# A kernel's start in finer slices, and five small moves of work behind it

## The chip, the cores and the metric

The kernel runs on one core of a Trainium2 chip. The metric is the device time of one execution in microseconds (us). Five engines are named below: PE (TensorE, the matmuls; PEld is its loading of weights), DVE (VectorE), ACT (ScalarE), POOL (GpSimd) and SP (SyncE, which here issues most of the loads). Each engine runs its own instruction list in order and waits on semaphores for the others.

## The reference, cut to what matters

The program is a two-layer backbone over 256 context tokens and 256 latent tokens of D = 1024 features. Layer 0 mixes tokens with a bidirectional chunkwise mLSTM, layer 1 with multi-head latent attention (MLA); each is followed by a gated convolutional feed-forward block (ConvFFN, 2816 features). Every sub-layer reads a modulated input and ends in a layer norm:

```python
def _modulation(cond, w, b):
    m = jax.nn.silu(cond) @ w + b
    return jnp.split(m[:, None, :], 6, axis=-1)

h = x * (1 + scale) + shift
x = _layer_norm(ALPHA * x + gate * sublayer(h), ln_g, ln_b)
```

The latent tokens are modulated by `c`, the context tokens by `c_ctx`, so there are two condition rows. The first product of all is `h @ m_w_up` (1024 x 2048 features for each of 512 tokens), and it needs `SiLU(c) @ ada_w`, a product with 1024 x 2048 weights (shift and scale), before its first operand exists. All arithmetic is fp32.

## The kernel before, in words

**Products.** A product in fp32 accuracy is three matmuls (`mm3`, lines 391 to 393): each operand is split in `hi`, its value rounded to the matmul type fp32r by a copy on ACT, and `lo = src - hi`, a subtraction on DVE; the sum is hi.hi, hi.lo, lo.hi. Activations are held by features on the 128 partitions with tokens along the row, in eight tiles of 128 features for D (`hT[k]`). Weights come through a ring (class `Stream`): SP loads raw tiles of 512 KB (`raw`), ACT casts them (line 330), DVE subtracts (line 333), and a use of the ring hands over the pair. The plan (`_plan`) fixes the order of the weights.

**What sets the order.** Outside the start the framework's scheduler orders each engine's instructions with the kernel's own generators in the background: `bg` is stepped by `tick` and finished by `drain`, `bg2` is a second list with the modulation of the later sub-layers, and `late` holds generators that `take_late` appends to `bg`. Their place in the text, and where a `yield` lets the product in front go on, is what moves work.

**The start** (`start_up`, within `manual_schedule`). `LOADS` is the order of the loads on SP: `a` is a group of modulation weights, `x` a group of tokens by feature tiles (`tokT`), `r` a whole weight tile of `m_w_up` (one tile of 128 output features, all 1024 input features). `STEPS` is the order of work on PE, DVE and ACT at once, one letter a step:
- `S`: cast and subtract one tile of modulation weights (`ada_split`, lines 396 and 397). `A`: its matmuls, with `SiLU(c)` and `SiLU(c_ctx)` as the four columns of a small operand (`condr`, hi and lo) against 512 columns of weights, line 472, result `adar`, four rows.
- `C`: copy of the rows; `T`: transposes of them to columns, line 484, result `adat`; `O`: bias added, giving shift and scale by partition (`mod0`).
- `E`: modulation of one feature tile of tokens (`mod_tile`); `H`: its split in hi and lo (`hT`).
- `W`: split of half a weight tile of `m_w_up`; `V` k m: the three matmuls of feature tile k into output tile m, 512 tokens wide, lines 391 to 393, result `up`. 8 x 5 of them are in the start (`NUP` = 5 output tiles), 120 matmuls.
- `D` n: n matmuls on zeros into a spare bank (line 664, result `idle`).

`GROUPS` says which feature tiles share one round of `A C T O`; before there are four groups of two. The small constants (`sm`) are loaded ahead of all in one transfer of 227 KB. `w_up` then goes on with the other 11 output tiles.

**The end of layer 0** (`w_fout0`). The second FFN product of layer 0 is built from partial products that are added on DVE (`u2`, `p5`, `p6`, `p7`, in PSUM and SBUF), lines 1436 to 1443 in two stages, while the last six weight tiles are split (line 333) and their operands `fz` are formed (line 1384).

**Layer 1's attention** (`mla`). The layer norm's output `z` is transposed (`ln_T`, line 1196, result `zT`), scaled with shift and scale by partition (line 1203 on ACT for even tiles, line 1205 on DVE for odd ones, result `zm`), and split (1208 and 1209, result `hl`). With `hl` PE makes the key-value rows `dkv` and the query rows `dq`; both get an RMS norm (`rms`, whose last scaling, line 1512, is on DVE). At the same time the norm's gain and bias are multiplied into `z` for the residual (`ln_x`, lines 1224 and 1225, from `late`), and the keys and values of the context, `kn` and `v`, are made and split.

**The second FFN** (`after0`, then `ffn_in`). The norm after the attention goes the same way, `ln_rows` (1168, 1170), `ln_T`, result `h`. `ffn_in` takes the pair of each weight against `h`: the hi weight against hi and lo of `h` side by side in 512 columns (a view `both` with hi and lo in two places of a tile), the lo weight against the 256 hi columns, in turn for each of the eight feature tiles (line 1317).

## Time and profile before

| what | value |
|---|---|
| median of three executions | 1374.81 us (1374.66 to 1375.21) |
| the profiled execution | 1372.7 us, of which 1370.9 us are its span |
| PE busy | 1346.8 us, 98% of the span; 24.1 us not busy |
| DVE, ACT, POOL busy | 1077.0, 720.9, 121.5 us |
| granted TensorE clock, mean | 0.998 of full speed |
| bytes moved | 297.58 MB, mean 217 GB/s |

The span is from the first to the last instruction that the hardware profiler saw in one execution; the profiled execution's own time holds a little more, before and behind. A row of the timeline reads: start and length in us, engine, line, operation, result <- operands, shape, how many in a row, and in brackets the idle time before it with what ended it. A row of the waits reads: who waited, for what, then us in total, times and the longest. Matmuls overlap: a length in a row is the time from a matmul's start to its modelled end, so the pace is the distance of two starts.

### The profile page before, as it was taken

What the parts mean: (1) busy time and instruction counts of PE and PEld (TensorE: products, weight loads), DVE (VectorE), ACT (ScalarE), POOL (GpSimd) and SP (SyncE); (2) the same over time, 40 slices, a digit from 0 to 9 for tenths busy, and PEclk for the clock granted to TensorE, in tenths of its full rate; (3) what the DMA queues carried; (4) which work ended last, traced back from release to release, by engine and by line L of the source; (5) the groups of instructions that cost most, each with busy time, mean ns of one, the idle gap of its engine ahead of it and who ended that gap; (6) DMA issues with size and microseconds to landing.
All of it is one profiled execution on the core that took longest, in us unless ns stands there. A gap on an engine that the chain in (4) does not pass through costs nothing.

```text
span 1370.9 us, 18618 instructions
## 1 busy us (share of the span) xinstructions
PE 1346.8 (98%) x6581; PEld 1121.5 (82%) x6581; DVE 1077.0 (79%) x1748; ACT 720.9 (53%) x1242; POOL 121.5 (9%) x215
## 2 busy tenths in 40 slices
PE   7999999999999999999999999999999999999997
PEld 3788888888788888888898888888878898888886
DVE  7699757677588696897979978767888889788873
ACT  6675444445544455464643343333557667466660
POOL 0122000011011011030001000000001001000100
PEclk9999999999999999999999999999999999999999
DMA  9789848789666363786627877745987436366760
GB/s 337 242 304 331 275 158 247 236 291 297 216 197 210 108 231 123 248 277 242 204 97 240 301 244 224 226 144 202 310 267 238 138 101 216 102 187 189 252 199 31
DMA packets 97900, 297.58 MB, mean 217 GB/s; under 512 B 12136, under 2 KB 24808, under 8 KB 97808
## 3 DMA queue, kind: packets, MB, share of 16 engines
q1 hardware_dynamic: 68672, 218.52, 48.4%
q0 software_dynamic: 17472, 57.57, 13.4%
q10 hardware_dynamic: 11664, 20.32, 4.1%
q8 instruction: 51, 0.84, 0.2%
q14 instruction: 41, 0.34, 0.1%
HBM read 262.90 MB, written 33.46 MB: 216 GB/s over the span
## 4 chain that ended last, share of the span: by engine, by line
PE 92%; DVE 3%; DMA 2%; ACT 1%; issue 1%; ACTq 0%; SPq 0%; DVEq 0%
PE fin L1317 8%; PE fin L392 6%; PE fin L391 6%; PE fin L393 6%; PE tok L391 6%; PE tok L392 6%; PE tok L393 6%; PE y L392 6%; PE y L393 6%; PE y L391 6%; PE qk L391 4%; PE qk L393 4%; PE qk L392 4%; PE up L391 2%; PE up L392 2%; PE up L393 2%
## 5 line engine op out<-in xcount | busy, mean ns | idle before, releaser
L333 DVE TENSOR_TENSOR w<-raw,w 128x1024 fp32r<-128x1024 f32 (+2 forms) x286 | 343.1, 1202 | 146.3 <-ACT w L330 141.5
L330 ACT CAST w<-raw 128x1024 fp32r<-128x1024 f32 (+2 forms) x286 | 296.2, 1037 | 287.9 <-PE tok L393 79.6
L512 DVE SCALAR_TENSOR_TENSOR junk<-ar,bc 128x1024 f32<-128x1024 f32 x128 | 155.7, 1216 | 4.7 <-ACT bc L554 2.4
L392 PE MATMUL fin<-h,w 128*128 128x512 f32 (+1 forms) x376 | 141.2, 376 | 0.0
L393 PE MATMUL fin<-h,w 128*128 128x512 f32 (+1 forms) x376 | 140.9, 375 | 0.0
L391 PE MATMUL fin<-h,w 128*128 128x512 f32 (+1 forms) x376 | 140.8, 376 | 0.1
L1317 PE MATMUL fin<-h,w 128*128 128x256 f32 (+1 forms) x640 | 112.9, 339 | 0.0
L1317 PEld LDWEIGHTS fin<-h,w 128*128 128x128 f32 x640 | 98.1, 189 | 14.6
L391 PE MATMUL qk<-xc,w 128*128 128x512 f32 x256 | 100.7, 393 | 0.0
L393 PE MATMUL qk<-xc,w 128*128 128x512 f32 x256 | 99.9, 390 | 0.0
L392 PE MATMUL qk<-xc,w 128*128 128x512 f32 x256 | 99.8, 390 | 0.0
L392 PEld LDWEIGHTS fin<-h,w 128*128 128x128 f32 x376 | 70.8, 188 | 13.1 <-DVE h L1209 0.2
L391 PEld LDWEIGHTS fin<-h,w 128*128 128x128 f32 x376 | 70.6, 188 | 13.2 <-ACT h L1208 0.3
L393 PEld LDWEIGHTS fin<-h,w 128*128 128x128 f32 x376 | 70.8, 188 | 12.6
L391 PEld LDWEIGHTS qk<-xc,w 128*128 128x128 f32 x256 | 48.1, 188 | 10.0 <-issue 0.4
L393 PEld LDWEIGHTS qk<-xc,w 128*128 128x128 f32 x256 | 48.1, 188 | 9.9
L392 PEld LDWEIGHTS qk<-xc,w 128*128 128x128 f32 x256 | 48.1, 188 | 9.7
L391 PE MATMUL up<-hT,w 128*128 128x512 f32 x128 | 50.3, 393 | 0.1
L392 PE MATMUL up<-hT,w 128*128 128x512 f32 x128 | 50.0, 390 | 0.3 <-DVE hT L397 0.3
L393 PE MATMUL up<-hT,w 128*128 128x512 f32 x128 | 49.9, 390 | 0.0
L391 PE MATMUL tok<-w,hT 128*128 128x512 f32 x128 | 49.8, 389 | 0.0
L392 PE MATMUL tok<-w,hT 128*128 128x512 f32 x128 | 49.8, 389 | 0.0
(456 smaller groups left out, 3160.1 us busy)
## 6 DMA issues: line engine op xcount, KB each, us to landing
raw<-in_ws SPq DMA_DIRECT2D x287, 512.0 KB, 4.6
ar<-in_adaT SPq DMA_DIRECT2D x80, 512.0 KB, 4.7
adaw<-in_ada_w SPq DMA_DIRECT2D x32, 256.0 KB, 6.2
t2d<-raw ACTq DMA_DIRECT2D x13, 512.0 KB, 5.6
raw<-t2d SPq DMA_DIRECT2D x13, 512.0 KB, 5.3
raw<-in_ws POOLq DMA_DIRECT2D x13, 512.0 KB, 7.5
zr<-fd ACTq DMA_DIRECT2D x33, 128.0 KB, 4.2
xmd<-xr POOLq DMA_DIRECT2D x16, 256.0 KB, 4.6
```

The lines of the kernel that those rows point to most:

```text
L330: k.nc.scalar.copy(h[:, :cols], src)
L333: k.nc.vector.tensor_sub(l[:, :cols], src, h[:, :cols])
L391: mm(out, w[0], x[0], start=start, stop=False, skip_group_check=on)
L392: mm(out, w[0], x[1], start=False, stop=False, skip_group_check=on)
L393: mm(out, w[1], x[0], start=False, stop=stop, skip_group_check=on)
L512: nc.vector.scalar_tensor_tensor(o, w, 1.0, self.bc[j], op0=ALU.mult, op1=ALU.mult, accum_out=col[:, k, j:j + 1])
L1317: nc.tensor.matmul(o, a, b, start=k == 0 and i == 0, stop=k == 7 and i == 1)
```

## The change

In the start:
- Modulation weights and the first five output tiles of `m_w_up` are laid out on the host as whole tiles in the order of use: `ada0`, 16 tiles of 128 x 1024 with whole rows, and `up0`, eight tiles, one for each feature tile k, holding its 128 rows times the 640 columns of the five output tiles. Before, the modulation weights were read with rows of 1 KB out of the full matrix, and the five `m_w_up` tiles came one output tile at a time.
- `GROUPS` is (0), (1), (2, 3), (4, 5), (6, 7): the first two feature tiles have rounds of their own, of two tiles (S, A) each, with matmuls of 256 columns instead of 512. `A` is now the hi half of a tile's matmuls and `B` the lo half.
- Only 32 columns of the constants (the conditions and the modulation bias, `sm0`) are loaded ahead; the rest (`s`) comes behind the second weight slice.
- `W` k splits one slice of 640 columns; `V` k m reads its columns. `LOADS` and `STEPS` are written anew, with ten matmuls on zeros ahead of all (`WARM`) in place of the seven in `D4` and `D3`. The ring starts with output tile 5.

Behind it:
- `w_fout0`: the second stage of the sums is a background generator, stepped by the ticks of the last six weight tiles, instead of standing ahead of them.
- layer 1's norm before the attention: all eight scalings of `ln_T` on ACT (`both=False`). `rms`: the last scaling on ACT. `ln_x` is taken up behind the `dkv` product, no longer ahead of `mla`, and the step of the background that stood there is gone.
- layer 1's norm before the second FFN: `ln_T4`. The eight transposes of the first token tile go ahead, then five matmuls on a weight into a spare bank, then the eight transposes of the second; scalings alternate by pairs between ACT and DVE, each followed by its cast and subtraction, and nothing else of it is issued ahead of the first one.
- `ffn_in` of layer 1: seven matmuls with hi weights (512 columns), eight with lo weights (256 columns), and the last hi one, instead of in turn. hi and lo of `h1` lie side by side, so that the 512 columns are one run.

What PE does from the start to the first product of `w_up` (rows with a count are instructions in sequence; `adar` the modulation rows, `adat` their transposes, `idle` the matmuls on zeros, `up` the product, `w` its weights). Before:

```order
L472 MATMUL adar<-adas,condr 4x512 x16
L664 MATMUL idle<-zero 128x512 x4
L484 MATMUL adat<-ident,adarow 128x4 x4
L472 MATMUL adar<-adas,condr 4x512 x16
L664 MATMUL idle<-zero 128x512 x3
L391 MATMUL up<-hT,w 128x512
L392 MATMUL up<-hT,w 128x512
L393 MATMUL up<-hT,w 128x512
```

And now:

```order
L627 MATMUL idle<-zero 128x512 x10
L487 MATMUL adar<-adas,condr 4x256 x16
L500 MATMUL adat<-ident,adarow 128x4 x2
L487 MATMUL adar<-adas,condr 4x256 x16
L487 MATMUL adar<-adas,condr 4x512 x4
L500 MATMUL adat<-ident,adarow 128x4 x2
L487 MATMUL adar<-adas,condr 4x512 x4
L405 MATMUL up<-hT,w_182 128x512
L406 MATMUL up<-hT,w_182 128x512
L407 MATMUL up<-hT,w_183 128x512
```

The first `up` matmul stood behind 32 wide modulation matmuls and seven on zeros; it stands behind 32 narrow and 8 wide ones, with the ten on zeros ahead of all.

DVE at the end of `w_fout0` (`w` are the weight splits, `fz` the operands, `v` and `y` with `u` the sums of the second stage). Before:

```order
L1438 TENSOR_TENSOR y<-y,u_8483 128x512
L333 TENSOR_TENSOR w<-raw,w 128x1024
L1384 TENSOR_TENSOR fz<-zr,fz 128x512
L1442 TENSOR_TENSOR v<-y,v 128x512
L1443 TENSOR_TENSOR y<-y,u_8481 128x512
L1442 TENSOR_TENSOR v<-y,v 128x512
L1443 TENSOR_TENSOR y<-y,u_8483 128x512
L333 TENSOR_TENSOR w<-raw,w 128x1024
L1384 TENSOR_TENSOR fz<-zr,fz 128x512
```

And now:

```order
L1479 TENSOR_TENSOR y<-y,u_8503 128x512
L347 TENSOR_TENSOR w<-raw,w 128x1024
L1422 TENSOR_TENSOR fz<-zr,fz 128x512
L347 TENSOR_TENSOR w<-raw,w 128x1024
L1422 TENSOR_TENSOR fz<-zr,fz 128x512
L347 TENSOR_TENSOR w<-raw,w 128x1024
L1422 TENSOR_TENSOR fz<-zr,fz 128x512
L347 TENSOR_TENSOR w<-raw,w 128x1024
L1484 TENSOR_TENSOR v<-y,v 128x512
L1485 TENSOR_TENSOR y<-y,u_8501 128x512
L1422 TENSOR_TENSOR fz<-zr,fz 128x512
L347 TENSOR_TENSOR w<-raw,w 128x512
```

The four sums stood together behind one weight split; now four splits go ahead of the first two, and the other two follow the fifth.

DVE in layer 1's projections (`hl` the subtractions of the attention's input, `v` those of the context's values, `z` with `gr` and `br` the norm's gain and bias, `w` 128x768 the splits of `dq`'s weights). Before:

```order
L1209 TENSOR_TENSOR hl<-zm,hl 128x256 x8
L397 TENSOR_TENSOR v_9248<-v_9241,v_9248 128x512
L397 TENSOR_TENSOR v_9258<-v_9251,v_9258 128x512
L1225 TENSOR_TENSOR z<-z,br 128x512
L1224 TENSOR_TENSOR z<-z,gr 128x512 x2
L1225 TENSOR_TENSOR z<-z,br 128x512 x2
L1224 TENSOR_TENSOR z<-z,gr 128x512
L333 TENSOR_TENSOR w<-raw,w 128x768
```

And now:

```order
L1208 TENSOR_TENSOR hl<-zm,hl 128x256 x7
L411 TENSOR_TENSOR v_9268<-v_9261,v_9268 128x512
L1208 TENSOR_TENSOR hl<-zm,hl 128x256
L411 TENSOR_TENSOR v_9278<-v_9271,v_9278 128x512
L347 TENSOR_TENSOR w<-raw,w 128x768 x3
L1556 RECIPROCAL rs<-rs 128x1
```

Six products with gain and bias stood ahead of the first of these weight splits; now three splits follow the last subtraction, and the products come later.

The diff, cut to its core:

```diff
-GROUPS = ((0, 2), (2, 4), (4, 6), (6, 8))
-LOADS = [(c[0], int(c[1])) for c in "a0 a1 x0 r0 r1 r2 x1 r3 a2 r4 x2 a3 x3".split()]
+GROUPS = ((0, 1), (1, 2), (2, 4), (4, 6), (6, 8))
+WARM = 10
+LOADS = (
+    "a00 a01 a10 a11 a20 a21 x0 w0 x1 a22 a23 w1 s a30 a31 a32 a33 w2 x2 x3 a40 w3 a41 a42 a43 w4 x4 x5 x6 w5 x7 "
+    "w6 w7").split()
 STEPS = (
-    "S00 A00 S01 S02 S03 S10 A01 A02 A03 S11 C0 D4 T0 O0 S12 A10 A11 A12 S13 E0 E1 A13 D3 W00 H0 V00 H1 C1 W10 T1 O1 "
-    "V10 W20 E2 E3 H2 V01 H3 V11 V02 W30 W01 S20 W11 S21 V12 V20 V30 S22 V21 V22 V13 S23 V31 V32 W21 A20 A21 A22 W40 "
-    "A23 V23 C2 T2 V14 O2 S30 E4 W31 E5 H4 V03 V33 H5 V04 A30 V24 V40 S31 V50 S32 V51 A31 V41 A32 S33 V42 A33 V52 "
-    "W41 V53 C3 T3 O3 V43 E6 V44 V54 V34 H6 V60 V61 V62 E7 H7 V70 V71 V72 V63 V73 V74 V64").split()
+    "S00 A00 B00 S01 A01 S10 S11 B01 C0 T0 O0 A10 S20 A11 B11 B10 S21 A21 E0 C1 A20 T1 W0 H0 B20 B21 O1 S22 E1 "
+    "V02 S23 H1 W1 V01 S30 A22 V00 V04 B22 A23 B23 V03 V12 C2 A30 T2 B30 S31 V11 V14 O2 S32 S33 B31 E2 W2 A31 V10"
+    " A32 A33 E3 B32 H2 B33 S40 C3 V13 V21 H3 W3 V20 A40 T3 B40 V22 V31 S41 S42 V33 O3 W4 V34 V24 E4 V30 E5 V23 "
+    "B42 B41 A41 H4 A42 S43 W6 V44 A43 B43 V42 H5 V40 W5 V43 C4 T4 W7 O4 V51 E7 E6 V54 V50 V53 H7 V41 H6 V52 V62 "
+    "V73 V71 V32 V63 V60 V61 V72 V70 V64 V74").split()
...
-    for m in range(16):
+    for m in range(NUP, 16):
...
+    w0 = np.asarray(i["ada_w"][0]).reshape(8, 128, 6, D)[:, :, 0:2]
+    ada0 = []
+    for f0, f1 in GROUPS:
+        g = w0[..., f0 * 128:f1 * 128].transpose(1, 0, 2, 3).reshape(128, -1)
+        ada0 += [g[:, j:j + 1024] for j in range(0, g.shape[1], 1024)]
+
+    up0 = i["m_w_up"][0].reshape(8, 128, -1)[:, :, :NUP * 128]
...
-        for op, g in LOADS:
...
+        raw, tag = {}, [("raw", NRAW)] * 3 + [("ar", 2)] * 2 + [("ar1", 1), ("junk", 1), ("raw", NRAW)]
+        nw = NUP * 128
+        for step in LOADS:
+            op, n = step[0], [int(x) for x in step[1:]]
             if op == "a":
-                wd = 128 * (f1 - f0)
-                nk = 512 // wd
-                self.adaw[g] = []
-                for k in range(8):
-                    if k % nk == 0:
-                        t = self.uf("adaw")
-                        self.adaw[g].append(t)
-                    ap = bass.AP(tensor=src.tensor, offset=src.offset + k * 128 * 6 * D + f0 * 128,
-                                 ap=[[6 * D, 128], [D, 2], [1, wd]])
-                    c = k % nk * 2 * wd
-                    nc.sync.dma_start(t[:, c:c + 2 * wd].rearrange("p (a b) -> p a b", a=2), ap)
+                t = raw[step] = self.uf("adaw")
+                src = self.a["ada0"][sum(2 * (f1 - f0) for f0, f1 in GROUPS[:n[0]]) + n[1]]
...
+            for _ in range(WARM):
+                nc.tensor.matmul(idle, self.zero[:, 0:128], self.zero, start=True, stop=True)
...
-                    self.ada_mm(rows[g], n[1], parts.pop((g, n[1])))
+                    todo[g] -= 1
+                    self.ada_mm(rows[g], g, n[1], parts[g, n[1]][op == "B"], first, todo[g] == 0)
...
+                    self.split(w[g][0][:, :nw], w[g][1][:, :nw], raw["w%d" % g][:, :nw])
...
+                    c = slice(m * 128, (m + 1) * 128)
+                    self.mm3(ps[m], (w[k][0][:, c], w[k][1][:, c]), (hT[k][:, 0], hT[k][:, 1]),
                              made[m] == 0, made[m] == 7)
...
+    def ln_T4(self, zs, A, B, dst):
+        nc, pin = self.nc, self.tc.keep_in_program_order
+        w = self.st.hl[self.st.nu][0]
+        pts = [self.ps("zT") for _ in range(4)]
+        idle = self.ps("idle")
+        for t in range(2):
+            for k in range(8):
+                o = (k % 2) * 256 + t * 128
+                i = nc.tensor.transpose(pts[k // 2][:, o:o + 128], zs[t][:, k * 128:(k + 1) * 128], self.ident)
+                if t and not k:
+                    pin(i)
+            if not t:
+                for _ in range(IDLE):
+                    pin(nc.tensor.matmul(idle, w[:, 0:128], w[:, 0:512], start=True, stop=True))
+        def one(k):
+            c = slice((k % 2) * 256, (k % 2 + 1) * 256)
+            p, m = pts[k // 2][:, c], tmp[:, c]
+            hi, lo = dst(k)
+            if k // 2 % 2 == 0:
+                nc.scalar.activation(m, p, AF.Identity, bias=B[:, k:k + 1], scale=A[:, k:k + 1])
+            else:
+                nc.vector.tensor_scalar(m, p, A[:, k:k + 1], B[:, k:k + 1], op0=ALU.mult, op1=ALU.add)
+            i = nc.scalar.copy(hi, m)
+            nc.vector.tensor_sub(lo, m, hi)
+            return i.ins
+        tmp = self.s2("zm")
+        first = one(0)
+        for k in range(1, 8):
+            if k % 2 == 0:
+                tmp = self.s2("zm")
+            with self.tc.issue_after(first):
+                one(k)
+            if k % 2:
+                yield
...
-                    two = ps.rearrange("p (a t) -> p a t", a=2)
-                    for k in range(8):
-                        c = slice(k * 128, (k + 1) * 128)
-                        hi, lo = hT(k)
-                        if both is None or p < 2:
-                            self.mm3(ps[:, :n], (w[0][:, c], w[1][:, c]), (hi, lo), k == 0, k == 7)
-                            continue
-
-                        mms = [(two, w[0][:, c], both(k)), (ps[:, :n], w[1][:, c], hi)]
-                        for i, (o, a, b) in enumerate(mms if k < 7 else mms[::-1]):
-                            nc.tensor.matmul(o, a, b, start=k == 0 and i == 0, stop=k == 7 and i == 1)
+                    if both is None or p < 2:
+                        for k in range(8):
+                            c = slice(k * 128, (k + 1) * 128)
+                            self.mm3(ps[:, :n], (w[0][:, c], w[1][:, c]), hT(k), k == 0, k == 7)
+                    else:
+                        mms = [(0, k) for k in range(7)] + [(1, k) for k in range(8)] + [(0, 7)]
+                        for i, (x, k) in enumerate(mms):
+                            c = slice(k * 128, (k + 1) * 128)
+                            nc.tensor.matmul(ps[:, :n] if x else ps, w[x][:, c],
+                                             hT(k)[0] if x else both(k), start=i == 0, stop=i == 15)
...
-        for b in range(2):
-            nc.vector.tensor_tensor(u2[b], p6[b], u2[b], op=ALU.add)
-        for b in range(2):
-            nc.vector.tensor_tensor(p7[b], p7[b], u2[b], op=ALU.add)
-        for b in range(2):
-            v = self.s2("v")
-            nc.scalar.copy(v, p7[b])
-            nc.vector.tensor_tensor(v, p5[b], v, op=ALU.subtract)
-            nc.vector.tensor_tensor(p5[b], p5[b], u2[b], op=ALU.subtract)
-            vv.append(v)
+        def sums():
+            for b in range(2):
+                nc.vector.tensor_tensor(u2[b], p6[b], u2[b], op=ALU.add)
+            yield
+            for b in range(2):
+                nc.vector.tensor_tensor(p7[b], p7[b], u2[b], op=ALU.add)
+            yield
+            for b in range(2):
+                v = self.s2("v")
+                nc.scalar.copy(v, p7[b])
+                nc.vector.tensor_tensor(v, p5[b], v, op=ALU.subtract)
+                nc.vector.tensor_tensor(p5[b], p5[b], u2[b], op=ALU.subtract)
+                vv.append(v)
+                yield
...
+        self.bg.append(sums())
         for i in range(6):
             w = st.use(("y21", 0, i))
             prod(p1, "2", w, i, on=True)
             self.tick(1)
             operand()
+        self.drain()
...
-        nc.vector.tensor_scalar(dst, ps, ss, None, op0=ALU.mult)
+        nc.scalar.activation(dst, ps, AF.Copy, scale=ss)
...
         st.unhold("dkv")
-        self.tick()
+        self.take_late()
...
-            yield from k.ln_T(zs, A, B, dst, g == 1)
+            yield from (k.ln_T4(zs, A, B, dst) if l else k.ln_T(zs, A, B, dst, g == 1))
...
-            yield from k.ln_T(zs, A, B, hl if g else hc, g == 1)
+            yield from k.ln_T(zs, A, B, hl if g else hc, g == 1, False)
...
         k.drain()
-        k.take_late()
         att = k.mla(hl)
...
-        h1 = lambda i: tuple(h1u[i // 2][:, n, (i % 2) * 256:(i % 2 + 1) * 256] for n in range(2))
+        h1 = lambda i: tuple(h1u[i // 2][:, i % 2, n * 256:(n + 1) * 256] for n in range(2))
...
-        acts = k.ffn_in(1, h1, 256, 1, both=lambda i: h1u[i // 2][:, :, (i % 2) * 256:(i % 2 + 1) * 256])
+        acts = k.ffn_in(1, h1, 256, 1, both=lambda i: h1u[i // 2][:, i % 2])
```

109 lines of the change are left out of this document (48 added, 61 removed).

## The prediction

> **What bounds the kernel now.** I read the page first, then the waits of the matmul engine, then its order of time wherever it waited. The page's own lines:
>
> ```profile
> span 1370.9 us, 18618 instructions
> PE 1346.8 (98%) x6581; PEld 1121.5 (82%) x6581; DVE 1077.0 (79%) x1748; ACT 720.9 (53%) x1242; POOL 121.5 (9%) x215
> ```
>
> PE is busy for 1346.8 of 1370.9 us. A change of this size can win only in the 24 us in which PE stands still, or by making its matmuls follow each other more closely. The waits of PE, longest first (what waited, for whom; total, times, longest):
>
> ```profile
> PE adar L472 <- ACT adas L396: 6.7, 1, 6.7
> PE zT L1196 <- DVE z L1168: 1.7, 1, 1.7
> PE y L392 <- DVE w L333: 1.2, 2, 0.7
> PE dq L392 <- DVE w L333: 1.0, 1, 1.0
> PE dkv L391 <- ACT hl L1208: 0.6, 1, 0.6
> PE dkv L393 <- DVE hl L1209: 0.5, 1, 0.5
> PE fin L391 <- ACT h L1208: 0.4, 1, 0.4
> ```
>
> So there is one large hole, the start, and a handful of small ones, which all lie between 990 and 1180 us: the end of layer 0 and layer 1's attention and norm. Between 58 and 990 us PE never waits; whatever the start gains is carried through unchanged. The tail (PE's last 7 us of idle) is not touched.
>
> **The start.** PE in order of time (start, length, engine, line, result and operands, count, idle before):
>
> ```profile
> 6.70 1.01 PE L472 MATMUL adar<-adas,condr 128*4 128x512 f32 x2 [6.70 <-ACT adas L396]
> 20.34 0.49 PE L391 MATMUL up<-hT,w 128*128 128x512 f32 x1
> 21.15 0.50 PE L392 MATMUL up<-hT,w 128*128 128x512 f32 x1 [0.32 <-DVE hT L397]
> 57.37 0.39 PE L393 MATMUL up<-hT,w 128*128 128x512 f32 x1
> ```
>
> The last of the 120 matmuls of the start-up's 40 V steps begins at 57.37. From 22 us on PE runs without a hole, so its end is set by when the first V step is done and by how much modulation work was done before it. What it waits for until then is loads, then splits (cast on ACT, subtraction on DVE). The rate, in 40 slices of the first 60 us, from the view of the DMA queues:
>
> ```profile
> GB/s 0 199 263 300 354 327 360 358 352 348 374 412 404 401 401 376 348 350 348 383 388 359 350 349 343 379 400 415 404 407 254 284 25 0 0 0 0 175 63 243
> ```
>
> Three casts that waited for a load, and two subtractions, in order of time:
>
> ```profile
> 5.60 1.04 ACT L396 CAST adas<-adaw 128x1024 fp32r<-128x1024 f32 x1 [1.67 <-DMA adaw<-in_ada_w]
> 7.59 1.04 ACT L396 CAST adas<-adaw 128x1024 fp32r<-128x1024 f32 x1 [0.95 <-DMA adaw<-in_ada_w]
> 16.51 1.05 ACT L396 CAST adas<-adaw 128x1024 fp32r<-128x1024 f32 x1 [0.38 <-DMA adaw<-in_ada_w]
> 6.68 1.23 DVE L397 TENSOR_TENSOR adas<-adaw,adas 128x1024 fp32r<-128x1024 f32 x1 [2.13 <-ACT adas L396]
> 19.80 0.69 DVE L397 TENSOR_TENSOR w<-raw,w 128x512 fp32r<-128x512 f32 x1 [0.33 <-ACT w L396]
> ```
>
> From 7.59 to 16.51 six tiles of 512 KB arrive, in rows of 1 KB: 3.15 MB in 8.92 us, 353 GB/s. While x and up tiles (rows of 2 and 4 KB) come, the row reads 401 to 412. The new modulation tiles have rows of 4 KB and the new up tiles of 2.5 KB, so I take 400 GB/s for all of them.
> [...]
>
> New first V step: the row has moved 0.69 MB by 4.5 us, and the old first tile (227 KB of small constants and 512 KB) was cast 0.95 us after its 0.76 MB. The new one is complete after 0.54 MB, by the same row at 3.9, so at about 4.9. Five more tiles of 0.524 MB at 400 GB/s: the sixth at 11.5, x0 at 12.1, w0 at 12.9. ACT casts the sixth by 12.5, DVE subtracts it by 13.8, then come, in DVE's order, half of x0 (0.4), w0 with 640 columns (0.8, between the rows for 512 and 1024) and hT (0.7): 15.7. The first V step ends at about 16.2; before it ended at 21.7 (21.15, its idle gap of 0.33 to the next matmul and one of 0.23). That is 5.5 us earlier. But PE has then done less: before, 32 matmuls of 512 columns at 0.227 us, 7.3 us; now 32 of 256 at 0.120 and 8 of 512, 5.7 us (both paces below). Left: 3.9 us. The 10 matmuls on zeros lie before the first tile is split, in time in which PE stood still, and cost nothing unless they last past 6 us; the seven fillers in the old order stood before 20.34 and are in the 5.5 already. Later loads: 13.3 MB in all, the last (w7) at 4.9 + 12.8 / 0.4 = 36.9; its split stands on ACT and DVE ahead of the modulation of tiles 7 and 6, some 4.5 us, and 13 V steps of 0.68 us follow: 50.3, earlier than 53.8, so PE sets the end. I take **3.6 us**, 0.3 off for waits at single splits. Bounds: 1.5 and 4.8.
>
> **The sums at the end of layer 0** (w_fout0). DVE and then PE:
>
> ```profile
> 998.75 0.68 DVE L1442 TENSOR_TENSOR v<-y,v 128x512 f32<-128x512 f32 x1
> 1000.54 0.69 DVE L1443 TENSOR_TENSOR y<-y,u 128x512 f32<-128x512 f32 x1
> 1001.14 1.21 DVE L333 TENSOR_TENSOR w<-raw,w 128x1024 fp32r<-128x1024 f32 x1
> 1002.41 0.50 PE L392 MATMUL y<-w,fz 128*128 128x512 f32 x1 [0.70 <-DVE w L333]
> ```
>
> Four sums (2.4 us) stood ahead of the weight split for which PE then waited 0.70 us. In the new order three splits go ahead of them. A weight feeds 12 matmuls (2.7 us) and costs DVE 1.7 us with its operand, so the moved sums fit behind: **0.7 us**, bounds 0 and 0.9. The first wait at this line (1.2 less 0.7 in the list, 0.5) stands ahead of the sums in both orders and stays.
>
> **Layer 1's projections.** The norm's products with gain and bias now come after the last dq weight split has been ordered:
>
> ```profile
> 1072.39 1.28 DVE L1224 TENSOR_TENSOR z<-z,gr 128x512 f32<-128x512 f32 x2
> 1073.60 1.28 DVE L1225 TENSOR_TENSOR z<-z,br 128x512 f32<-128x512 f32 x2
> 1075.40 0.95 DVE L333 TENSOR_TENSOR w<-raw,w 128x768 fp32r<-128x768 f32 x1
> 1070.74 0.84 ACT L330 CAST w<-raw 128x768 fp32r<-128x768 f32 x1 [0.61 <-PE dkv L393]
> ```
>
> The cast was done at 71.6, the subtraction waited for six of those products until 75.4, and PE lost 0.95 us. Without them it follows the cast: **0.95 us**. They now stand ahead of the two reciprocals of the query norm: 3.6 us, covered by the 48 kn matmuls (48 x 0.12 = 5.8 us); the scaling of cq, moved from DVE to ACT, is late by what is left, so I charge **+0.2** (0 to 0.8).
> Before that, four of the eight scalings of hl move from DVE to ACT:
>
> ```profile
> 1062.79 1.50 ACT L1203 ACTIVATE zm<-zT,lnB,lnA 128x256 f32<-128x256 f32 x3
> 1065.37 0.37 ACT L396 CAST kn<-kn 128x256 fp32r<-128x256 f32 x1 [0.55 <-DVE kn L397]
> 1066.59 2.56 ACT L1208 CAST hl<-zm 128x256 fp32r<-128x256 f32 x8
> ```
>
> Four of 0.5 us would put the casts 2 us later, but in the new order only one more stands before the first cast (three follow it), in place of a wait of 0.55 us that ACT had there; and DVE, rid of four, reaches hl's subtractions sooner, for which PE waited 0.5 in the list. **0.3 us** gain, bounds -0.9 gain and +1.0 loss.
>
> **Layer 1's second norm** (ln_T4):
>
> ```profile
> 1175.45 1.57 PE L1196 MATMUL zT<-ident,z 128*128 128x128 f32 x12 [1.71 <-DVE z L1168]
> 1176.03 1.04 ACT L1203 ACTIVATE zm<-zT,lnB,lnA 128x256 f32<-128x256 f32 x2 [0.27 <-PE zT L1196]
> 1177.42 0.74 PE L391 MATMUL fin<-h,wu 128*128 128x256 f32 x4 [0.40 <-ACT h L1208]
> ```
>
> All eight transposes of the first row tile and five matmuls into a spare bank (1.1 us) now fill the 1.71 us wait. After 1175.45 the first operand needs one transpose, one scaling (0.55) and one cast (0.35) where two scalings went ahead: fin can start at about 1176.7. **0.75 us**; bounds 1.1, and a loss of 0.3 if the five end late.
>
> **The second FFN's first product.** 640 matmuls, alternately 512 and 256 columns, first in the chain of waits:
>
> ```profile
> 1189.35 112.78 PE fin L1317 x640
> ```
>
> Then two runs of one size, the first and the last row of each in PE's order of time (1050.63 to 1052.44: eight steps; 1052.67 to 1058.30: 47):
>
> ```profile
> 1050.63 0.39 PE L391 MATMUL y<-wu,fz 128*128 128x512 f32 x1
> 1052.44 0.39 PE L393 MATMUL y<-wu,fz 128*128 128x512 f32 x1
> 1052.67 0.28 PE L391 MATMUL kn<-ckT,wu 128*128 128x256 f32 x1
> 1058.30 0.28 PE L393 MATMUL kn<-ckT,wu 128*128 128x256 f32 x1
> ```
>
> 112.78 / 320 = 0.352 us for a pair. Runs: 1.81 / 8 = 0.226, and 5.63 / 47 = 0.120, together 0.346. Grouped as 7, 8 and 1, a tile of 16 matmuls takes 2.77 instead of 2.82 us, times 40: 1.9 us. I take **1.6**; lower bound 0, if the 512-column step is slower for its own sake (its operand is now contiguous, so it should not be).
>
> Sum: 3.6 + 0.7 + 0.95 - 0.2 + 0.3 + 0.75 + 1.6 = 7.7 us. The profiled execution (1370.9 span, 1372.7 in all) lies 2.1 under the median of 1374.81; I subtract from the median: **1367.1 us**.
>
> **The rivals.** (a) Loads at the old rate. Speaks for it: the slices before 6 us read 199 to 300 and the 1 KB rows held 353. Then w7 lands at 4.9 + 12.8 / 0.353 = 41.2, the start ends at 54.6 and single splits come late on the way: 2.0 instead of 3.6, 1368.7.
> (b) The waits of layer 1's projections only change their names: ACT, with 4 more scalings and 4 of the row norms, sets hl and cq late. For it: ACT's rows above show it two gaps only in ten microseconds, 0.55 and 0.61. Nothing from these terms and 1 us more: 1369.3 (7.7 less 1.05 less 1.1).
> (c) Slower: the order of the steps assumes arrivals, and W7 stands ahead of E7, E6, H7 and H6 on both engines. If the loads run at the 263 GB/s of the third slice throughout, w7 lands at 53.6, the start ends at 67.0, 9.6 us later than before, and with 4.1 gained elsewhere the time is 1380.3. It decides below about 296 GB/s; against it stand 24 slices at 343 and more.
> (d) The start does not move the end at all, because DVE is what w_up waits for; busy time of PE, PEld, DVE, ACT and POOL in one stretch of it:
>
> ```profile
> 80.00:90.00 10.00, 10.00 (x45) 8.26 (x45) 10.00 (x16) 7.86 (x15) 2.76 (x6) 1.00 0.92 304
> ```
>
> Then 4.1 us are left, 1370.7. Against it: PE has no wait there, and the evacuations move forward with it.
>
> **How the numbers follow.** Forecast 0.62; (a) 0.14; (b) 0.11; (c) 0.03; (d) 0.05; two or more terms failing together, 1371 to 1373, 0.05. A change of under 0.2%, 2.75 us, cannot be told from none here: faster means under 1372.06. That gives 0.90 faster, 0.07 within, 0.03 slower. The forecast's own range is 1364.8 (the start at its bound of 4.8, the hl scalings, the sums and the norm half-way to theirs) to 1368.9; with (a), (b) and (d) in it, and 0.4 of spread above (d), it is 1364.8 to 1371.1.
>
> **What would show it.** Right: the first up matmul near 15 us, the last of the start's 120 near 53.8 and no wait of PE over 0.6 us between them; no wait at line y after the first sum; the dq wait gone; fin starting 1.2 us after the last normalized piece; 640 matmuls in about 111 us. Wrong: waits for w or hT in the start after 20 us (rate or order), a wait at cqT or dkv longer than before (ACT), 640 matmuls still in 112.8 us.

## The result, and the profile after

The changed kernel takes 1366.07 us (median of four executions, 1365.58 to 1366.54), the kernel before beside it 1374.74 (four, 1373.44 to 1375.21). The ratio is 0.994 with a 95% interval of 0.9928 to 0.9953, so 6.5 to 9.9 us faster; the forecast was 7.7 us, 1367.1 in a range of 1364.8 to 1371.1. The two profiled executions are 7.1 us apart (spans 1370.9 and 1363.8). All terms below are read in these two traces and not in the medians, which are 8.7 us apart: the profiled execution of before was 2.0 us below its median, that of after 0.5. Up to the last product the terms come to 7.34 us; behind the last matmul the changed kernel takes 0.24 us more, which leaves the 7.1.

From the page of the changed kernel:

```profile
span 1363.8 us, 18639 instructions
PE 1347.3 (99%) x6605; PEld 1125.5 (83%) x6605; DVE 1073.6 (79%) x1738; ACT 725.3 (53%) x1251; POOL 121.9 (9%) x215
```

PE has as much to do as before (1346.8 us then); what went is its standing still. Its waits after (who, for what, us in total, times, longest), the ones that answer to the list of before:

```profile
PE adar L487 <- ACT adas L410: 0.8, 1, 0.8
...
PE s L405 <- ACT qn L1747: 0.6, 1, 0.6
...
PE y L406 <- DVE w L347: 0.4, 1, 0.4
...
PE zT L1223 <- DVE z L1167: 0.3, 1, 0.3
PE dkv L405 <- ACT hl L1207: 0.3, 1, 0.3
```

The 6.7 us at the start, the 1.7 at `zT` and the 1.0 at `dq` are gone. One large wait is new: `s`, the scores, for `qn` from ACT. The start in order of time:

```profile
1.49 3.87 PE L627 MATMUL idle<-zero 128*128 128x512 f32 x10 [1.49 <-DVE adav L470]
6.18 0.64 PE L487 MATMUL adar<-adas,condr 128*4 128x256 f32 x4 [0.81 <-ACT adas L410]
...
10.51 3.19 PE L487 MATMUL adar<-adas,condr 128*4 128x256 f32 x20
...
14.90 0.49 PE L405 MATMUL up<-hT,w 128*128 128x512 f32 x1
15.63 0.50 PE L406 MATMUL up<-hT,w 128*128 128x512 f32 x1 [0.23 <-DVE hT L411]
```

The first `up` matmul is at 14.90 instead of 20.34, and behind 15.63 PE has no wait over 0.1 us until the end of layer 0. Rate of the loads in 40 slices of the first 60 us, which read 327 to 374 between 6 and 16 us before, while modulation tiles came:

```profile
GB/s 0 63 317 415 415 429 408 391 402 410 390 401 410 407 400 390 412 391 407 421 380 389 392 395 406 413 410 287 320 265 79 0 177 259 371 388 371 361 180 254
```

**Where the time went.** The same matmul can be found in both traces, and the difference of its two starts is the gain up to that place. The table has this gain at nine places for all kernels of this study (us): the first matmul of the token product (117.44 in the kernel before), the first `dkv` matmul for the context (1037.96), the first `dq` (1074.94), the first `kn` behind it (1085.20), the first score (1106.36), the first `o` (1119.05), the second norm's first transpose (1172.60), the second FFN's grouped matmuls (1189.18), and the first matmul behind them (1301.96). Between the first column and 690 us it moves by less than 0.1, so differences above 0.1 between kernels mean something where the program is the same up to there; at the end of layer 0 they do not (below).

| kernel | tok | dkv | dq | kn | s | o | zT | fin | y |
|---|---|---|---|---|---|---|---|---|---|
| changed | 3.99 | 5.06 | 5.62 | 6.68 | 6.13 | 5.73 | 5.70 | 6.30 | 7.34 |
| changed, again | 4.07 | 4.32 | 4.89 | 5.98 | 5.43 | 5.03 | 5.02 | 5.62 | 6.66 |
| warm0_alt | 2.32 | 2.48 | 3.03 | 4.08 | 3.52 | 3.13 | 3.11 | 3.69 | 3.70 |
| rows1k_oldlay | 1.13 | 1.26 | 1.82 | 2.89 | 2.25 | 1.86 | 1.84 | 2.44 | 3.48 |
| pairs_sums | 2.42 | 2.27 | 2.84 | 3.93 | 3.38 | 2.98 | 2.97 | 3.55 | 4.59 |
| smfirst_idle0 | 0.34 | 0.57 | 1.14 | 2.23 | 1.68 | 1.28 | 1.27 | 0.79 | 1.83 |
| rms_dve | 3.98 | 4.60 | 5.22 | 6.49 | 3.34 | 2.79 | 2.77 | 3.38 | 4.42 |
| late_before | 3.99 | 4.59 | 5.16 | 1.59 | 1.60 | 1.61 | 1.57 | 2.17 | 3.21 |
| both_lnT | 4.02 | 5.16 | 5.55 | 6.64 | 6.08 | 5.65 | 5.64 | 4.77 | 5.81 |
| late_scores | 4.22 | 4.13 | 4.71 | 5.78 | 5.72 | 5.73 | 4.44 | 5.04 | 6.08 |
| late_pool | 3.97 | 5.01 | 2.62 | 3.00 | 3.01 | 3.00 | 2.96 | 3.56 | 4.60 |
| warm14 | 4.26 | 4.10 | 4.67 | 5.73 | 5.18 | 4.73 | 4.72 | 5.33 | 6.37 |
| smfirst_warm14 | 2.94 | 3.06 | 3.62 | 4.71 | 4.16 | 3.76 | 3.75 | 4.35 | 5.39 |

The first row by terms, with the forecast in brackets: start 3.99 (3.6), end of layer 0 1.07 (0.7), `hl` 0.56 (0.3), `dq` 1.06 (0.95), queries and scores -0.95 (-0.2), second norm 0.60 (0.75), second FFN's product 1.04 (1.6).

### The profile page after: what moved, and what is told of

It reads as the page before. It is cut to its first block, busy times and chain, and to the rows that moved or that the text cites. A ratio compares the mean times of both kernels' runs of the same rounds, so it can differ in the third digit from the quotient of the medians.

```text
span 1363.8 us, 18639 instructions
## 1 busy us (share of the span) xinstructions
PE 1347.3 (99%) x6605; PEld 1125.5 (83%) x6605; DVE 1073.6 (79%) x1738; ACT 725.3 (53%) x1251; POOL 121.9 (9%) x215
## 4 chain that ended last, share of the span: by engine, by line
PE 95%; DVE 2%; ACT 1%; DMA 1%; issue 1%; SPq 0%; DVEq 0%; ACTq 0%
PE fin L1354 8%; PE y L406 6%; PE fin L405 6%; PE y L407 6%; PE fin L406 6%; PE fin L407 6%; PE y L405 6%; PE tok L405 6%; PE tok L407 6%; PE tok L406 6%; PE qk L405 4%; PE qk L407 4%; PE qk L406 4%; PE up L406 2%; PE up L405 2%; PE up L407 2%
## 5 line engine op out<-in xcount | busy, mean ns | idle before, releaser
L407 PEld LDWEIGHTS fin<-h,w 128*128 128x128 f32 x376 | 70.8, 188 | 12.7
```

Of the source, the lines that this page charges most:

```text
L407: mm(out, w[1], x[0], start=False, stop=stop, skip_group_check=on)
```

## The experiments

Several kernels carry two edits in places far apart; each is read at its own columns.

**The zeros ahead of the start, and the order in the second FFN.**

```diff
-WARM = 10
+WARM = 0
...
-mms = [(0, k) for k in range(7)] + [(1, k) for k in range(8)] + [(0, 7)]
+mms = [(x, k) for k in range(7) for x in (0, 1)] + [(1, 7), (0, 7)]
```

> The changed kernel with two edits far apart, each read at its own place in the trace. (1) The ten matmuls on zeros ahead of the start are left out. My theory: they are not free filling, they take PE's slow first microseconds: the ten took 3.87 us, 0.43 us for 512 columns at first, where 512 columns take 0.227 later. Without them the 16 narrow matmuls of the first round run at about twice 0.12 us, the rows of the first feature are ready 1.0 us later, and the first up matmul starts at 15.7 to 16.0 instead of 14.90; the gain carried out of the start falls from 3.97 to 3.0 to 3.5 us. Rival, as the prediction had it: they cost and bring nothing, 14.90 and 3.97 stay within 0.1. (2) The second FFN's product in turn again (512, 256, 512 ... columns), hi and lo still side by side. If the grouping made the gain there, the 640 matmuls take 112.7 to 112.9 us again; if the contiguous operand made it, they stay at 111.7.

One execution, 1369.21. PE at the start:

```profile
6.28 1.02 PE L487 MATMUL adar<-adas,condr 128*4 128x256 f32 x4 [6.28 <-ACT adas L410]
...
11.02 5.09 PE L487 MATMUL adar<-adas,condr 128*4 128x256 f32 x20
...
17.17 0.39 PE L405 MATMUL up<-hT,w 128*128 128x512 f32 x1
```

The row of twenty holds sixteen narrow matmuls (256 columns) and four wide ones (512). They take 5.09 us, where the changed kernel needs 3.19 with its waits in them: by the distances of their starts, 0.21 and 0.43 us instead of 0.12 and 0.23, PE runs at about half its pace up to 16 us. The first `up` matmul is at 17.17, 2.27 late, and 1.67 of the start's 3.99 us are lost, more than my theory said; the rival falls. The second edit, in the chain of waits of four kernels, in this order: before, changed, this one, and the next one (old layout, new order):

```profile
1189.35 112.78 PE fin L1317 x640
```

```profile
1183.04 111.74 PE fin L1354 x640
```

```profile
1185.65 112.78 PE fin L1354 x640
```

```profile
1186.91 111.74 PE fin L1356 x640
```

The order makes all of the 1.04 us, the contiguous operand nothing.

**Rows of 1 KB, and the old layout of h1.** Each modulation tile is read as four pieces of 256 columns; hi and lo of `h1` lie in two places again.

```diff
+if op == "a":
+    t, src = t.rearrange("p (a b) -> p a b", a=4), src.rearrange("a p b -> p a b")
 nc.sync.dma_start(t, src)
...
-h1 = lambda i: tuple(h1u[i // 2][:, i % 2, n * 256:(n + 1) * 256] for n in range(2))
+h1 = lambda i: tuple(h1u[i // 2][:, n, (i % 2) * 256:(i % 2 + 1) * 256] for n in range(2))
```

> The changed kernel with two edits. (1) The modulation tiles lie in memory so that a tile is read in rows of 1 KB, four for each partition, all else the same. If the row length set the rate (353 against 400 GB/s), the six tiles, x0 and w0 that the first V step needs land 1.1 us later, the first up matmul starts at about 15.9, waits at single splits follow, and the start keeps 2.4 to 3.0 of its 3.97 us. If rows of 1 KB are as good, nothing moves by more than 0.1. (2) hi and lo of h1 in two places of the tile again, the grouped order kept: 111.7 us for the 640 matmuls if the order alone made the gain, 112.2 or more if the contiguous run did.

One execution, 1369.54. The rate, and the last wait of PE in the start:

```profile
GB/s 0 39 290 371 353 346 348 352 380 375 348 364 365 348 349 345 372 380 358 369 349 348 369 383 388 395 411 404 404 366 232 391 123 11 183 257 344 339 341 352
```

```profile
41.79 0.63 PE L487 MATMUL adar<-adas,condr 128*4 128x512 f32 x2 [0.29 <-DVE adas L411]
```

345 to 380 GB/s while these tiles come, as in the kernel before; the first `up` matmul is at 16.29 (expected 15.9), PE waits for splits as late as 41.79, and 1.13 us of the gain are left, less than I expected (2.4 to 3.0). The row length is a condition of the start's gain, and its price, 2.86 us, is larger than the 1.4 us at the first V step. In the mean of the slices from 4.5 to 33 us the changed kernel reads 404 GB/s and this one 359, with the same bytes in the same order.

**Modulation by pairs, and the sums in front.** The first two feature tiles share one round of four weight tiles; the steps are kept, the first round's C, T and O left out and E0 put behind the common O. The sums of `w_fout0` run before the last six weight tiles.

```diff
-GROUPS = ((0, 1), (1, 2), (2, 4), (4, 6), (6, 8))
+GROUPS = ((0, 2), (2, 4), (4, 6), (6, 8))
...
-self.bg.append(sums())
+for _ in sums():
+    pass
```

> The changed kernel with two edits. (1) The first two feature tiles of modulation in one round of four weight tiles with 512 columns, as groups of two before; loads, splits, slices and the order of the steps otherwise kept. My theory: the start is paced by the splits (DVE stands without a gap from 6.16 to 15.5 us, six subtractions of 1.22 us and the first modulation, weight and operand), and the steps put six tiles ahead of the first V in both cases, so the single rounds are worth little: first up matmul at 14.9 to 15.4, 3.5 to 4.0 us kept. Rival: modulation by single feature tiles is what lets the product start early; then two more tiles at 1.3 us stand ahead of it, 17.5, and about 1.4 us are kept. (2) The sums of layer 0's end in front of the weight splits again. The prediction took their wait at its idle time, 0.70 us. The trace says 0.97: a matmul after a wait begins 0.23 us later than its idle time shows, and the one behind it 0.11 late. So from the first fz matmul with a wait to the first dkv matmul 0.95 us are lost if that reading is right, 0.7 if the idle time is the price.

One execution, 1368.33. PE's first `up` matmul, then ACT behind the common O:

```profile
16.25 0.49 PE L399 MATMUL up<-hT,w 128*128 128x512 f32 x1 [1.21 <-ACT hT L404]
```

```profile
14.46 0.60 ACT L581 ACTIVATE xT<-xT,mod 128x256 f32<-128x256 f32 x1 [1.43 <-DVE mod L505]
14.97 0.71 ACT L404 CAST w<-raw 128x640 fp32r<-128x640 f32 x1
15.59 0.61 ACT L404 CAST hT<-xT 128x512 fp32r<-128x512 f32 x1
```

My theory falls, and so does the rival's number: 2.42 us are kept, 1.57 lost, in the middle between 3.5 and 1.4. The six subtractions do pace the path, one every 1.28 us, and the loads set that pace with them: five of the six casts wait 0.22 to 0.25 us for their tile. But with single rounds the first tile's shift and scale are ready before the sixth is done; with a common round the modulation (0.60), the weight's cast and the operand's cast come one after the other behind the last of them. The sums in front bring back a second wait (0.69 at 1000.13, after one of 0.61 at 993.67), and the gain goes from 2.42 to 2.27 over this stage. What that is worth needs the section on the repeated run.

```profile
1000.13 0.50 PE L400 MATMUL y<-w,fz 128*128 128x512 f32 x1 [0.69 <-DVE w L341]
```

**All constants first, and no matmuls in the second norm's wait.**

```diff
-    "a00 a01 a10 a11 a20 a21 x0 w0 x1 a22 a23 w1 s a30 ...
+    "s a00 a01 a10 a11 a20 a21 x0 w0 x1 a22 a23 w1 a30 ...
...
-IDLE = 5
+IDLE = 0
```

> The changed kernel with two edits. (1) The other 211 KB of small constants are loaded ahead of the modulation tiles, as before. If the loads pace the first steps, all of them come 0.5 us later (0.211 MB at 400 GB/s): first up matmul at 15.4, 3.4 to 3.6 us kept; if the queue's beginning is bound by its issues and not by bytes, less than 0.2 is lost. (2) The five matmuls on a weight between the two halves of the second norm's transposes are left out. My theory: they fill a wait and bring nothing, fin starts within 0.1 us of before. Rival: they keep PE at its pace, and without them the eight transposes and the first fin matmuls are slower by 0.3 us or more.

One execution, 1371.11. PE at the start, a stage of it in the view by windows (busy time of PE, PEld, DVE, ACT, POOL, granted clock, DMA share, GB/s), and PE at the second norm:

```profile
1.49 4.63 PE L627 MATMUL idle<-zero 128*128 128x512 f32 x10 [1.49 <-DVE adav L470]
...
13.05 5.02 PE L487 MATMUL adar<-adas,condr 128*4 128x256 f32 x20
```

```profile
14.00:16.00 2.00, 2.00 (x12) 1.12 (x9) 2.00 (x2) 1.51 (x2) 0.00 (x0) 1.00 1.04 411
```

```profile
1174.18 1.78 PE L1223 MATMUL zT<-ident,z 128*128 128x128 f32 x8 [1.49 <-DVE z L1167]
1175.71 1.22 PE L405 MATMUL fin<-h,wu 128*128 128x256 f32 x4
1176.73 0.41 PE L406 MATMUL fin<-h,wu 128*128 128x256 f32 x1
```

The ten zeros were there, but none of them ran at full pace (4.63 us), and PE stayed at half pace to 18 us; the first `up` matmul is at 19.14 and 3.65 us are lost. This mixes two causes; the last run parts them. Note that the granted clock reads 1.00 in that stage: it does not show this half pace, the distance of two starts does. At the second norm the same thing: behind the wait the eight transposes take 1.78 us instead of 1.25 and the `fin` matmuls stand 0.21 us apart instead of 0.12 for two microseconds. From the transposes to the grouped matmuls the kernel loses 0.48 us against before where the changed one gains 0.60. The rival was right: the five matmuls are worth 1.08 us here, and not by filling a wait. In none of the eleven traces with the five does the pace fall at this place.

**The RMS scaling on DVE.**

```diff
-nc.scalar.activation(dst, ps, AF.Copy, scale=ss)
+nc.vector.tensor_scalar(dst, ps, ss, None, op0=ALU.mult)
```

> The changed kernel with the last scaling of the RMS norms on DVE again. In the changed kernel a new wait stands where PE begins the scores (s, for qn from ACT, 0.65 us; 0.55 us of the gain are lost there). Theory A: the norm's products with gain and bias, taken up later, push DVE's work on the queries, and with it ACT's; then the wait stays at 0.5 to 0.7 here and the whole time within 0.3 us. Theory B: ACT is late because it has the scalings; then the wait falls under 0.2, and the gain at the scores is 6.6 instead of 6.1.

```profile
PE kn L406 <- DVE ckT L1610: 2.3, 1, 2.3
...
PE s L405 <- ACT qn L1747: 0.6, 1, 0.6
```

One execution, 1368.58. The wait at the scores stays at 0.6, which theory A forecast; but a wait of 2.3 us that neither theory had stands ahead of it: the scalings now queue on DVE behind the products with gain and bias, and the transposed keys (`ckT`) with them. I had booked this move as a small loss (+0.2); the later products need it: with them it is worth 2.5 us (gain from `dkv` to `o` +0.67 with it, -1.81 without).

**The products with gain and bias taken up ahead of the attention.**

```diff
-self.take_late()
+self.tick()
...
+k.take_late()
 att = k.mla(hl)
```

> The changed kernel with the norm's products with gain and bias taken up ahead of the attention again (and the step of the background behind the dkv product). By the prediction DVE is then late with dq's weight split: PE's wait of 0.95 us at dq comes back and costs 1.06 (what the two traces differ by there). Rival: eight scalings on ACT and the RMS scalings there have emptied DVE enough, the wait is under 0.3. By theory A of the run before, the wait at the scores goes away, and the net loss is 0.4 to 0.6 us; if it stays, 1.0.

```profile
PE ckT L1605 <- ACT ckr L1557: 2.2, 1, 2.2
...
PE dq L406 <- DVE w L347: 0.8, 1, 0.8
```

One execution, 1369.72. The wait at `dq` is back (0.8), and the one at the scores is gone (gain 1.59 at `kn`, 1.60 at `s`): it comes from the later products. The net loss is 4.1 us up to the scores, not 0.5, because of `ckT` again: the row norm on ACT waits 0.96 us for its reciprocal, which stands on DVE behind the products. The kernel before had neither edit and no such wait.

**Four scalings back on DVE, and the old second norm.**

```diff
-yield from k.ln_T(zs, A, B, hl if g else hc, g == 1, False)
+yield from k.ln_T(zs, A, B, hl if g else hc, g == 1)
...
-yield from (k.ln_T4(zs, A, B, dst) if l else k.ln_T(zs, A, B, dst, g == 1))
+yield from k.ln_T(zs, A, B, dst, g == 1)
```

> The changed kernel with two edits far apart. (1) Four of the eight scalings of hl back on DVE: the waits at dkv return (0.31 becomes 0.65, and 0.46 at the third matmul), 0.55 to 0.65 us between the transposes and the first dq matmul; under 0.2 if the later products with gain and bias had made that gain. (2) The second norm's transposes by the old function, without the five matmuls: PE's stretch from its first transpose to the product of the second FFN is 0.6 us longer, as in the kernel before. If PE's pace falls in the wait as it did without the five matmuls (first fin matmuls 0.21 us apart instead of 0.12 for 2.4 us), it is up to 1.7 us longer.

```profile
1169.81 2.59 PE L1195 MATMUL zT<-ident,z 128*128 128x128 f32 x12 [1.70 <-DVE z L1167]
1172.28 1.22 PE L405 MATMUL fin<-h,wu 128*128 128x256 f32 x4
```

One execution, 1367.22. From `dkv` to `dq` 0.39 us are gained instead of 0.56: with the products out of DVE's way the scalings on ACT are worth only 0.17. But `late_before`, with the scalings on ACT and the products ahead of the attention again, has 0.57 there: either of the two edits alone brings most of this gain. From the transposes to the grouped matmuls it is 0.87 slower than before, 1.47 worse than the changed kernel: twelve transposes take 2.59 us, and 1.57 in the profile of before with the same order and the same wait of 1.7. So of the two traces of the old order one pays for PE's pace and the other does not.

**The changed kernel again.**

> The changed kernel unchanged, for what differs between executions of one program. Theory: two things in its trace are luck of the execution and not of the change: when PE comes to its full pace in the start (in this trace within the ten matmuls on zeros, in other kernels right behind them, in one not before 18 us), and the first wait at the end of layer 0 (0.40 us here, 0.5 to 1.1 in the others, where the loads of zr come late). Then this profile has the start's gain anywhere from 2.3 to 4.0 us and that wait at another value, and the executions spread over 1.5 us or more. Rival: these hang on the program; then both come out as before within 0.1, and the executions spread by under 1 us.

Median of five executions 1366.42 (1365.95 to 1369.36), before 1374.18 (nine); ratio 0.9948, 0.9934 to 0.9961. One row of its waits:

```profile
PE y L406 <- DVE w L347: 1.1, 1, 1.1
```

The length of the first wait at the end of layer 0 is luck of the execution: 1.1 us instead of 0.4, and the gain over that stage 0.25 instead of 1.07, with the same program. Over all twelve executions in which the sums are in the background, it is -0.16 to 1.14, median 0.24; with the sums in front (one execution) -0.15. The forecast's 0.7 is within that, but one trace could not have settled it. The first wait is 0.54 and 0.61 us in the two traces with the sums in front and 0.40 to 1.12 in the twelve with them behind, so whether the new order itself makes it longer in some executions is open. What makes it long is seen in part: ACT forms `fz` from `zr`, and ahead of the wait it stands idle for loads of `zr` (1.12 and 0.31 us in the first trace, 1.36 and 0.38 in this one). When PE comes to its full pace differs too: within the ten zeros in four of the nine executions with ten (3.87 to 4.50 us for the ten), right behind them in three, at 7.3 us in one and at 18 in one. One of the nine timed executions of the changed kernel, 1369.36, is 3 us above the median, about what a late rise costs (2.60 us between the two starts with all constants first, 0.34 and 2.94 of the gain); that it was one is not shown.

**The products with the scores, and fourteen zeros.**

```diff
-self.take_late()
...
+self.take_late()
...
 Ps[h] = scores(h)
+self.tick()
...
-WARM = 10
+WARM = 14
```

> The changed kernel with two edits. (1) The norm's products with gain and bias are taken up only with the scores, one piece behind each of the first heads, so that DVE has none of them between the dkv product and the queries. By theory A the wait at the scores (0.65 us) and the lost gain behind it (6.68 to 5.73 us between qr and o) go away: gain at o 6.4 to 6.7, 0.7 to 0.9 us faster than the changed kernel, unless the pieces delay the heads' maxima and exponentials, for which PE then waits: from o to the norm's transposes up to 1 us longer. [...]

```profile
1128.84 0.39 PE L405 MATMUL o<-PT,v 128*128 128x256 f32 x1 [0.47 <-ACT PT L410]
1139.27 0.39 PE L405 MATMUL o<-PT,v 128*128 128x256 f32 x1 [0.90 <-ACT PT L410]
```

Median of five 1366.74 (1365.92 to 1366.84), ratio 0.9946 (0.9933 to 0.9958): no difference from the changed kernel that can be told. The 0.95 us between `kn` and `o` come back as forecast (5.78 and 5.73), and 1.29 go from `o` to `zT`: DVE has no room among the heads either. What the products delay is seen in DVE's second rotary step of the queries, in the changed kernel and in this one:

```profile
1097.30 0.69 DVE L1567 TENSOR_TENSOR qr<-qr,rp 128x512 f32<-128x512 f32 x1
```

```profile
1096.03 0.68 DVE L1567 TENSOR_TENSOR qr<-qr,rp 128x512 f32<-128x512 f32 x1
```

The first `qr` matmul is at 1085.27 and 1086.18, so the step ends 12.7 us behind it in the changed kernel and 10.5 here, as in the kernel before. In the changed kernel ACT then casts a weight ahead of the second `qrs` and of `qn`, for which PE waits; here both go ahead of that cast.

**The products on POOL.**

```diff
-nc.vector.tensor_tensor(zs[t][:, c], zs[t][:, c], g[h], op=ALU.mult)
-nc.vector.tensor_tensor(zs[t][:, c], zs[t][:, c], b[h], op=ALU.add)
+e = nc.gpsimd if ln == 1 else nc.vector
+e.tensor_tensor(zs[t][:, c], zs[t][:, c], g[h], op=ALU.mult)
+e.tensor_tensor(zs[t][:, c], zs[t][:, c], b[h], op=ALU.add)
```

> The changed kernel with the products with gain and bias of layer 1's norm on POOL instead of DVE, in the same place of the program. POOL is busy for under 2 of 15 us there. Theory A: DVE is free for the queries, the wait at the scores goes, 0.5 to 0.9 us faster than the changed kernel. Rival: POOL and DVE hinder each other where they work at one time; then DVE's rows there become longer (a subtraction of 128x512 takes 0.68 us now) and PE waits as before or longer, 0 to 2 us slower.

```profile
1062.92 7.72 DVE L1208 TENSOR_TENSOR hl<-zm,hl 128x256 fp32r<-128x256 f32 x7
```

```profile
1061.96 2.71 POOL L1264 TENSOR_TENSOR z<-z,br 128x512 f32<-128x512 f32 x2
...
1068.99 1.37 POOL L1264 TENSOR_TENSOR z<-z,br 128x512 f32<-128x512 f32 x1
```

Median of five 1368.76 (1368.51 to 1370.21), ratio 0.9965 (0.9952 to 0.9979): about 2.5 us slower than the changed kernel. Between `kn` and `o` nothing is lost, as theory A has it; but seven subtractions of `hl` take 7.72 us beside POOL's products, 1.1 each, where the changed kernel needs 0.35:

```profile
1062.30 1.76 DVE L1208 TENSOR_TENSOR hl<-zm,hl 128x256 fp32r<-128x256 f32 x5
```

POOL's last product ends at 1070.36 and the seventh subtraction at 1070.64; the eighth, at 1071.17 with no product beside it, takes 0.41 us, as the one at 1066.19 in the changed kernel does. The `hl` rows are long where POOL's products run; two subtractions of `v` at 1061.71, beside them too, take 1.29 us as in the changed kernel, so which rows POOL delays, and by what, is not shown.

**Fourteen zeros alone, and with all constants first.**

```diff
-WARM = 10
+WARM = 14
```

> The changed kernel with fourteen matmuls on zeros in place of ten and nothing else. In the run with both edits the gain carried out of the start was 4.2 us instead of 4.0, with the first up matmul at 14.68. Theory: the four more keep PE at work until the first split is there, so that its full pace comes before the first round in nearly every execution; start gain 4.1 to 4.3, five executions within 1.2 us of each other, median 0.1 to 0.4 us below the changed kernel's 1366.1 to 1366.4, which is less than can be told. Rival: the phase of the pace is luck with fourteen as with ten; one start in eight or so is 2 to 3 us longer.

> The other constants (211 KB) loaded ahead of the modulation tiles, with fourteen matmuls on zeros. In the run with ten, the first up matmul stood at 19.14 and 3.6 us of the start's gain were lost, with PE at half its pace up to 18 us. If that pace made most of it, PE is at its full pace here by 7.5 us, the first up matmul at 16.0 to 17.3 (the second tile's cast was 2.45 us late there, which is the loads' part), and the start keeps 1.5 to 2.5 us. If the loads made it, the first up matmul is at 18.5 or later and under 0.8 us is kept.

Fourteen alone: median of five 1366.13 (1365.77 to 1366.56), ratio 0.994 (0.9926 to 0.9953), the first `up` matmul at 14.66, 0.2 to 0.3 us more kept in the start. It is not told apart from the changed kernel; that it makes a late rise rarer fits (none of ten timed executions with fourteen stands as much as 1 us above their medians) and is not shown. With all constants first:

```profile
7.23 0.63 PE L487 MATMUL adar<-adas,condr 128*4 128x256 f32 x4 [0.83 <-ACT adas L410]
...
15.97 0.50 PE L405 MATMUL up<-hT,w 128*128 128x512 f32 x1
```

One execution, 1367.52. PE is at full pace in the first round (0.63 us for four), everything comes 1.05 us later, and 2.94 of the start's gain are kept. So the small constants cost 1.0 to 1.3 us of the 3.65 in the earlier run, and PE's pace the rest.

## Why the prediction was right, point by point

- **The total.** 7.7 us forecast, 8.7 between the medians, 7.8 between those of the repeated run, 7.3 by the terms of the two traces. That the sum comes so close is in part luck: start, end of layer 0, `hl` and `dq` came out 0.39, 0.37, 0.26 and 0.11 better, queries and scores, second norm and second FFN 0.75, 0.15 and 0.56 worse. The lower end of the range, 1364.8, is what the sum gives with the bounds in full; half-way, as the words say, it gives 1365.3. The measured median lies above both.
- **The start.** First `up` matmul "near 15" (14.90), end of the first V step at 16.2 (15.96 and 0.24), 3.6 us (3.99 and 4.07). The chain of the estimate, loads at 400 GB/s, cast, subtraction, modulation, operand, is what the trace shows. Going back to rows of 1 KB, to pairs or to all constants first costs 1 to 3 us each (2.86, 1.57 and 1.3): none of the three changes is spare. One step was wrong, though the sum hid it: that the ten matmuls on zeros "cost nothing". The sum used 0.120 us for a narrow matmul, and with them the changed kernel has it from the first round on; in the run without them it is 0.21 up to 16 us, and 1.67 us are lost.
- **The end of layer 0.** 0.7 forecast, 1.07 and 0.25 in two executions of one program. The second wait is gone in every run with the moved sums, as forecast. It was priced at its idle time, 0.70, and by starts it cost more: the matmul behind it and the next one start 1.09 and 0.34 us behind the one before instead of 0.23, which makes 0.97. The first wait, taken as fixed at 0.5, moves between 0.4 and 1.1. The term was right in kind; its size is not settled, and the bounds (0 to 0.9) held neither the 1.07 nor, in other traces, a loss of 0.16.
- **`hl` and `dq`.** 0.3 and 0.95; measured 0.56 and 1.06. For `hl` the mechanism holds, DVE reaches the subtractions sooner, but the forecast saw one of two ways to it. Before, four scalings and one product of 0.68 us (at 1066.12) stood ahead of them on DVE; taking off the scalings alone gives 0.57 (late_before), the products alone 0.39 (both_lnT), both 0.56.
- **The scaling of cq on ACT, -0.2.** The step that failed most. I looked for the lateness at `cq`; it comes 15 us later, at the scores, and costs 0.95 us in all, outside the bounds of 0 to 0.8. Its cause is not the scaling on ACT but the same products with gain and bias, which push DVE's work on the queries and ACT's behind it: three runs that put them elsewhere have no loss there (late_before, late_scores, late_pool), and in each DVE's rotary step ends 10.5 us behind the first `qr` matmul; the one that takes the scaling off ACT keeps the wait, with the step at 12.4. So the later products bring 1.06 us at `dq` and take back 0.95 at the scores: together 0.11, where 0.75 was forecast.
- **The second norm.** 0.75 forecast, 0.60 in both executions. The five matmuls keep PE's pace, which the estimate did not have; against the one execution in which the old order lost it, the change is worth 1.47.
- **The second FFN's product.** 1.6 of 1.9 forecast, 1.04 measured and the same to 0.01 in every run with that order. The mechanism (alternation costs) is right, the size is not: grouped, a tile takes 111.74 / 40 = 2.79 us, not the 2.77 of two pure runs. The trace has it in the wide matmuls: the eight of a tile take 1.84 us by their starts, not 1.81, and the eight narrow ones 0.95, as forecast. Why is open.
- **The rivals.** (a) is what the kernel does when its rows are cut to 1 KB, and then costs 2.9 us, not 1.6. (b), waits that only change their names, came true for the queries alone, and not by ACT's load. (c) and (d) did not come about.

## What to carry to other kernels

The gain of a stage is best read as the difference of the starts of the same matmul in two traces: it holds to 0.1 us where the program between is the same, and it shows a loss (the scores) that the sum of the gains hides. Ask of each matmul on zeros whether PE is at full pace without it, from the distance of starts and not from the granted clock (1.00 from 14 to 16 us in the run with narrow matmuls 0.21 us apart). And moves that were made together may be one move: the later products brought 1 us at `dq` only together with the RMS scaling on ACT; with one of the two taken back, 2.5 and 4.1 us of the gain were lost.

## What the runs showed of the hardware

At the start and behind two waits PE ran at about half its pace: 512 columns 0.43 us apart instead of 0.227, 256 columns 0.21 instead of 0.12, 128 columns 0.21 instead of 0.11. In the starts with zeros it mostly left the half pace three to six microseconds after its first matmul, at a point that differs between executions of one program (the ten zeros took 3.87 and 4.09 us in the two traces of the changed kernel; in one other kernel it came only at 18 us). Without the five matmuls it fell back to the half pace in a wait of 1.5 to 1.7 us, in two of three traces, and left it 3.7 to 4.0 us behind the first transpose after the wait. What sets the point of the rise, and why the pace falls in one such wait and not in another, is not shown.
